# Moving one general path to the front of a branch in a mixture-of-experts kernel

## The chip, the cores and the metric

The kernel runs on one core of a Trainium2 chip. The core has a matrix engine (TensorE, PE in the rows), a vector engine (VectorE, DVE), a scalar engine (ScalarE, ACT), a general engine (GpSimd, POOL) and a sync engine (SyncE, SP) that issues most transfers. Each engine has an instruction queue of its own and runs through it in order; engines wait for one another by semaphores. The metric is the device time of one execution in microseconds (us), as the median of several.

## The reference

Two model blocks run one after the other on 256 tokens of width 1024. The first has a pooling and attention mixer and a gated feed-forward layer, the second a state-space and mLSTM mixer and then a hierarchical mixture of experts with 32 experts, of which each token takes two. The change concerns the experts:

```python
pg, g_sel = lax.top_k(p_group, 1)
e_in = jnp.take_along_axis(e_logits, g_sel[:, :, None], axis=1)[:, 0]
top_v, top_i = lax.top_k(e_in, TOP_K)
gates = jax.nn.softmax(top_v, axis=-1) * pg
ids = (g_sel * EXPERTS_PER_GROUP + top_i).reshape(-1).astype(jnp.int32)
order = jnp.argsort(ids)
tok = order // TOP_K
xs = xf[tok]
sizes = jnp.bincount(ids, length=N_EXPERTS).astype(jnp.int32)
hg = lax.ragged_dot(xs, w_gate.astype(xs.dtype), sizes)
hu = lax.ragged_dot(xs, w_up.astype(xs.dtype), sizes)
ys = lax.ragged_dot(jax.nn.silu(hg) * hu, w_down.astype(xs.dtype), sizes)
ys = ys * gates.reshape(-1)[order][:, None].astype(ys.dtype)
y = jax.ops.segment_sum(ys, tok, num_segments=t)
```

So for each expert the tokens that chose it are gathered, multiplied by its gate and up weights (1024 x 512 each) and its down weights (512 x 1024), scaled, and added back into the tokens' rows. How many tokens an expert gets is known only at run time. With these inputs 26 of the 32 experts get any; six of them get over 32 tokens (107, 85, 50, 50, 46 and 33), none over 256.

## The kernel before

Until about 555 us the dense parts run, as straight code. The expert stage that follows is in `experts`. The experts are put in an order at run time (`compact`): first those fixed at the front, whose weights are loaded early, then the rest, and the places are chosen so that a heavy expert stands second in a pair. The program runs over the pairs; `nest` stops it after the last expert that has tokens.

A **round** (`enter`) works on up to 32 tokens (CAP) of one expert: 16 products of the gathered tokens with the four gate and up weight tiles (L1851, into the PSUM tile gu or, for a further round, gx), with the turn (L1885, a transposition) and the down products (L1896) of the round before it woven in between; then ScalarE and VectorE form silu(gate) x up (L1867 to L1874), and TensorE adds the earlier round's result into the output sums (`flush`, L1799). Every four experts one `gather` (L1743, L1765, L1772) collects the tokens of their first 32 places. So the last half of a round is done within the next round.

A **pair** runs the first round of its experts a and b. Then `key[p]`, read from a tile by all engines, decides. If it is at most 32 (CAP), control goes to the Else of L2038, where SyncE issues the next weight loads. If it is over 32 (an *over pair*: here pairs 4 to 9) and at most 256 (T), the second expert's further rounds run (`rounds`, one after the other, each behind a test at L1960 whether there are more tokens, up to round RI = 4, and from there a general loop). If it is over 256, which the keys bring about only where the pair's *first* expert has over 32 tokens, the Else of L2039 runs the general path, `rest`: a loop with a run-time count, for a and for b. Here it never runs, but its code stands between the rounds and the join, and the rounds end with a jump over it. The tests of L2038 and L1960 have a branch hint, issued by `enter` early in the round (L1822); the test of L2039 has none.

The engines meet each of these tests separately, in their own queues. At a join every engine has to have its semaphore counts the same whichever way was taken; the way that leaves a block out sets marks for it.

`order` (L1690 to L1698) makes the keys: two very small products that carry the counts into the chosen order, and four VectorE instructions that write the tiles ce (counts) and ekey (keys). It runs in the first gather, ahead of its last part.

Of the kernel before, what the change touches and what calls it, by code (L numbers as in the profile page):

```python
# [16 lines left out]
ALU = mybir.AluOpType  # L17
# [8 lines left out]
T = 256  # L26
# [9 lines left out]
CAP = 32  # L36
# [62 lines left out]
class Kern:  # L99
# [1526 lines left out]
    def compact(self):  # L1626
# [13 lines left out]
        kt = self.ep.tile([1, NE // 2], F32, name="ekt", bufs=1)  # L1640
# [5 lines left out]
        V = nc.vector  # L1646
# [43 lines left out]
        def order():  # L1690
            for j, src in enumerate((cc, ec[:, 0:1])):
                nc.tensor.matmul(pp[0:1, 64 + 32 * j : 96 + 32 * j], src, P, start=False, stop=True, skip_group_check=True)
            V.tensor_copy(self.ce, pp[0:1, 64:128].rearrange("p (b e) -> p b e", b=2))

            first, second = (pp[0:1, 64:96].rearrange("p (q k) -> p k q", k=2)[:, j, :] for j in range(2))
            V.tensor_scalar(kt, first, float(CAP), 2.0 * T, op0=ALU.is_gt, op1=ALU.mult)
            V.tensor_tensor(kt, kt, first, ALU.max)
            V.tensor_tensor(self.key, kt, second, ALU.max)  # L1698

# [12 lines left out]
        def gates():  # L1712
            pg = self.pmi.tile([128, 512], F32, tag="mi", name="cmpg")
            nc.tensor.matmul(pg[0:NE, 0:T], P2, gT[0 : 64 + NE, :], start=True, stop=True, skip_group_check=True)
            self.split_gates(NE, pg)

        return sizes, places, order, moved, gates

    def gtile(self, name, shape, dt):
# [185 lines left out]
    def experts(self, st):  # L1905
        nc, tc = self.nc, self.tc
# [24 lines left out]
        sizes, places, order, moved, gates = self.compact()  # L1931
        parts = groups[0]
        chosen = parts[0]()
# [2 lines left out]
        self.counts()  # L1936
        places()
        parts[2]()
        order()
        parts[3]()  # L1940

        routing = {
            0: self.ranks, 1: lambda: self.gates(chosen),
        }

        def count(src, after=()):

            loads, vals = nc.values_load_multi_w_load_instructions(src, engines=[PE_, ACT_, DVE_, SP, POOL_])
            for ld in loads:
                for a in after:  # L1950
                    self.behind(ld, a)
            return vals[0], loads

        def loads(i, first, n):
            for q in range(6 * i + first, 6 * i + first + n):
                self.eload(NSLOT + q)

        def rounds(i, r, val, tag, prev, before=()):

            with tc.If(val > CAP * r, label=f"{tag}_{r}") if r > 1 else contextlib.nullcontext():  # L1960
                if r == RI:
                    end(i)
                    rest(i, r, val)
                    clear()
                    return
                n = CAP * (r + 1)

                odd = r % 2 == (0 if i < GR else 1)

                s0 = GR * CAP if i < GR else 2 * CAP * (i % GR)  # L1970
                xh = self.xs[:, :, s0 : s0 + 2 * CAP]
                if not odd:
                    for f in self.gather(i, 1, r, 2 * CAP, xh, selh):
                        f()
                xs = xh[:, :, CAP:] if odd else xh[:, :, 0:CAP]
                marks = self.enter(i, r, xs, {}, (f"{tag}_{r + 1}", val > n) if n < T else None, prev)
                for m in marks:
                    for b in before:
                        self.behind(m, b)
                rounds(i, r + 1, val, tag, i)  # L1980

        def end(i):

            self.turn()
            m = self.down(i)
            self.flush()
            return m

        def rest(i, r, val):

            ro = self.roff
            nc.vector.tensor_copy(ro[:, 0:1], self.iotap[:, r : r + 1])
            nc.vector.tensor_scalar(ro[:, 1:2], self.iotap[:, 0:1], 0.0, float(CAP * r), op0=ALU.mult, op1=ALU.add)
            s0 = GR * CAP if i < GR else 2 * CAP * (i % GR)
            xh = self.xs[:, :, s0 : s0 + CAP]
            with tc.For_i(CAP * r, val, CAP):
                for f in self.gather(i, 1, None, CAP, xh, selh[:, :, :, 0:CAP]):
                    f()
                self.enter(i, None, xh)
                end(i)  # L2000
                nc.vector.tensor_scalar(ro, ro, float(CAP), None, op0=ALU.add)

        def clear():

            for h in range(2):
                nc.vector.tensor_scalar(self.st[:, 128 * h : 128 * h + 128], self.ones, 0.0, None, op0=ALU.mult)

        key = {}
        self.ereg = None

        def pair(p):

            a, b = 2 * p, 2 * p + 1
            if a in groups and a:

                for f in groups[a][1:]:
                    f()
            for i in (a, b):
                s0 = CAP * i if i < GR else 2 * CAP * (i % GR)
                marks = self.enter(  # L2020
                    i, 0, self.xs[:, :, s0 : s0 + CAP], {} if i else routing,
                    (f"over{p}", key[p] > CAP if p else "LikelyTaken") if i == a else None, i - 1 if i else None,
                )
                if i == 0:
                    moved()
                    gates()
                    self.rank = self.rank2
                    key[0], _ = count(self.key[0:1, 0:1])
                if i == a and i:
                    loads(i - 1, 4, 2)  # L2030
            if b + 1 in groups:
                groups[b + 1][0]()
            before = ()
            if b + 1 < NE:
                key[p + 1], before = count(self.key[0:1, p + 1 : p + 2], marks)
            ereg = self.ereg

            with tc.If(key[p] > CAP, label=f"over{p}") as c:  # L2038
                with tc.If(key[p] <= T) as c2:  # L2039

                    loads(a, 0, 6)
                    rounds(b, 1, key[p], f"over{p}", b, before)
                    loads(b, 0, 4)
                with c2.Else():
                    self.ereg = ereg
                    ca, cb = (count(self.ce[0:1, 0, i : i + 1])[0] for i in (a, b))
                    end(b)
                    rest(a, 1, ca)
                    loads(a, 0, 6)
                    rest(b, 1, cb)  # L2050
                    clear()
                    loads(b, 0, 4)
            with c.Else():
                self.ereg = ereg
                loads(a, 0, 6)
                loads(b, 0, 4)
            self.ereg = None
# [11 lines left out]
        def nest(p):  # L2069

            if p == NE // 2:
                last(NE - 1)
                return
            with tc.If(key[p] > 0) as c:  # L2074
                pair(p)
                nest(p + 1)
            with c.Else():
                last(2 * p - 1)


        for p in range(GR // 2):
            pair(p)
# [247 lines left out]
```

## Time and profile before

| | |
|---|---|
| median of 3 runs | 1009.46 us (1008.82 to 1010.08) |
| the profiled execution | 1012.31 us |
| its span, first to last instruction | 1010.3 us |
| mean granted TensorE clock | 0.929 of full speed |
| TensorE busy | 889.5 us, 88% |
| VectorE busy | 581.9 us, 58% |
| ScalarE busy | 428.5 us, 42% |
| moved by DMA | 252.19 MB, 250 GB/s |

Busy time is the time in which an engine has an instruction in work; branches, semaphore instructions and register work don't count. A wait is the idle time ahead of an instruction, put down to what released it. "PEq", "DVEq" and "ACTq" are the instruction queues (sequencers) of the engines, whose branch instructions have rows of their own. A branch on PE that takes long shows in its duration; on ScalarE and VectorE the time shows between the compare and the next instruction of the queue.

### The profile page before, as it was taken

How to read it: one execution, taken by the hardware profiler on the slowest of the kernel's cores; microseconds unless marked ns; L12 is line 12 of the kernel's file. 1: busy time of each engine (PE TensorE's matmuls, PEld its weight loads, DVE VectorE, ACT ScalarE, POOL GpSimd, SP SyncE). 2: the span in 40 equal slices, each digit the busy share in tenths (PEclk: the TensorE clock that was granted, in tenths of full speed). 3: DMA queues.
4: the chain of work that ended last, by engine and by line, in shares of the span. 5: the costliest groups of instructions: out<-in, count | busy, mean ns of one | idle time of the engine just before them, and what ended most of it. 6: DMA issues, size and time to landing. Idle time of an engine off the chain costs nothing. (4 is left out here: it accounts for less than half of the span.)

```text
span 1010.3 us, 17831 instructions
## 1 busy us (share of the span) xinstructions
PE 889.5 (88%) x6738; PEld 655.6 (65%) x6738; DVE 581.9 (58%) x1203; ACT 428.5 (42%) x788; POOL 135.4 (13%) x160
## 2 busy tenths in 40 slices
PE   7989999999999899999999888788687977797973
PEld 7969899999998799889998323244234323224332
DVE  6777888777776999988974432332232322323322
ACT  5445566655573656765545221211221321322313
POOL 3440331111115400161230000000000000000000
PEclk9999999999998999999999898887797987987987
DMA  8533445555564345435777599999484798997951
GB/s 341 204 119 126 167 159 189 208 198 202 179 235 177 126 151 191 160 116 199 291 291 264 199 407 418 423 417 415 179 334 169 316 363 330 374 378 296 390 239 48
DMA packets 36323, 252.19 MB, mean 250 GB/s; under 512 B 4144, under 2 KB 4272, under 8 KB 6320
## 3 DMA queue, kind: packets, MB, share of 16 engines
q1 hardware_dynamic: 35712, 249.51, 63.9%
q8 instruction: 83, 1.36, 0.5%
q14 instruction: 96, 0.79, 0.2%
q10 hardware_dynamic: 432, 0.53, 0.1%
HBM read 269.95 MB, written 1.05 MB: 268 GB/s over the span
## 5 line engine op out<-in xcount | busy, mean ns | idle before, releaser
L136 DVE TENSOR_TENSOR wlo<-ring,whi 128x1024 fp32r<-128x1024 f32 (+1 forms) x157 | 197.6, 1260 | 43.3 <-ACT whi L134 41.5
L134 ACT ACTIVATE whi<-ring 128x1024 fp32r<-128x1024 f32 (+1 forms) x160 | 167.7, 1052 | 123.1 <-PE up L153 19.1
L1902 DVE TENSOR_TENSOR y<-py,y 128x512 fp32r<-128x512 f32 x35 | 24.2, 692 | 192.4 <-ACT y L1901 184.5
L1851 PE MATMUL gu<-early,xs 128*32 128x512 f32 x472 | 81.0, 649 | 3.3 <-DVE ez L1868 3.3
L1765 PE MATMUL xsp<-sel,H 128*128 128x256 f32 (+1 forms) x224 | 41.3, 359 | 40.1 <-issue 20.9
L1886 ACT ACTIVATE hT<-py 128x128 f32<-128x128 f32 x35 | 9.7, 278 | 155.7 <-PE py L1885 155.7
L1851 PE MATMUL gu<-ring,xs 128*32 128x512 f32 x336 | 62.1, 638 | 10.3 <-issue 7.5
L1765 PEld LDWEIGHTS xsp<-sel,H 128*128 128x128 f32 x224 | 39.2, 268 | 43.2 <-issue 22.1
L1901 ACT ACTIVATE y<-py 128x512 fp32r<-128x512 f32 x35 | 20.9, 598 | 93.9 <-PE py L1896 93.9
L1772 DVE TENSOR_TENSOR xs<-xsp,gn 128x512 f32<-128x512 f32 (+1 forms) x30 | 19.1, 637 | 65.0 <-PE xsp L1765 48.2
L1851 PE MATMUL gu<-ringc,xs 128*32 128x512 f32 x160 | 34.5, 709 | 16.3 <-DMA ring<-in_we_dram 14.8
L152 PE MATMUL dn<-ah,whi 128*128 128x256 f32 x176 | 48.6, 276 | 0.0
L153 PE MATMUL dn<-al,whi 128*128 128x256 f32 x176 | 48.6, 276 | 0.0
L154 PE MATMUL dn<-ah,wlo 128*128 128x256 f32 x176 | 48.6, 276 | 0.0
L739 POOL TENSOR_TENSOR av<-sg,cc 128x256 f32<-128x256 f32 x22 | 30.5, 1387 | 126.7 <-ACT sg L737 126.2
L1799 PEld LDWEIGHTS eacc<-y,oneh 64*128 64x128 f32 x280 | 23.9, 188 | 34.9 <-ACT ez L1838 26.8
L1799 PE MATMUL eacc<-y,oneh 64*128 64x512 f32 x280 | 43.2, 426 | 1.3 <-ACT y L1901 1.2
L1868 DVE TENSOR_TENSOR ez<-gu,ez 64x512 f32<-64x512 f32 x35 | 23.9, 683 | 25.7 <-ACT ez L1867 25.5
L1885 PEld LDWEIGHTS py<-idr,ez 32*128 32x128 f32 x140 | 12.0, 145 | 40.4 <-issue 28.7
L732 DVE SCALAR_TENSOR_TENSOR cc<-u,cpack,cc 128x255 f32<-128x255 f32 (+1 forms) x88 | 37.4, 485 | 0.2
L1869 ACT ACTIVATE esz<-ez,col 32x512 f32<-32x512 f32 x35 | 25.2, 721 | 25.5 <-DVE ez L1868 25.5
L1874 DVE SCALAR_TENSOR_TENSOR ez<-ez,col,esz 32x512 f32<-32x512 f32 x35 | 25.9, 741 | 13.2 <-ACT esz L1869 10.7
(1220 smaller groups left out, 2693.8 us busy)
## 6 DMA issues: line engine op xcount, KB each, us to landing
ring<-in_wd_dram SPq DMA_DIRECT2D x77, 1024.0 KB
early<-in_we_dram SPq DMA_DIRECT2D x72, 1024.0 KB
ring<-in_we_dram SPq DMA_DIRECT2D x48, 1024.0 KB
ringc<-in_we_dram SPq DMA_DIRECT2D x32, 1024.0 KB
ringb<-in_we_dram SPq DMA_DIRECT2D x16, 1024.0 KB
xbuf<-in_we_dram SPq DMA_DIRECT2D x8, 1024.0 KB
ring<-in_wd_dram SPq DMA_DIRECT2D x4, 512.0 KB
xbuf<-in_xT_dram SPq DMA_DIRECT2D x4, 256.0 KB
```

Of the source, the lines that this page charges most:

```text
L134: nc.scalar.activation(hf[:, c], src[:, c], AF.Copy)
L136: eng.tensor_tensor(lf[:, c], src[:, c], hf[:, c].bitcast(F32), ALU.subtract)
L152: nc.tensor.matmul(ps, hi[:, j, :], xh, start=start, stop=False, skip_group_check=True)
L153: nc.tensor.matmul(ps, hi[:, j, :], xl, start=False, stop=False, skip_group_check=True)
L154: nc.tensor.matmul(ps, lo[:, j, :], xh, start=False, stop=stop, skip_group_check=True)
L732: nc.vector.scalar_tensor_tensor(cc[:, s, sh:T], in0=u[:, s, 0 : T - sh], scalar=self.c("cw", tap * 44 + m), in1=cc[:, s, sh:T], op0=ALU.m ...
L739: nc.gpsimd.tensor_tensor(a, sg, cc[:, 1, :], ALU.mult)
L1765: m = nc.tensor.matmul(ps[:, c * n * S : (c + 1) * n * S], self.H[j][:, b, ch], sel[:, b].rearrange("p k s -> p (k s)"), start=(b == 0 and ...
L1799: self.nc.tensor.matmul(self.sums[b][h], self.st[rows, b * 128 : b * 128 + 128], y[rows, :], start=False, stop=False, skip_group_check=True,)
L1851: m1 = nc.tensor.matmul(gu[32 * t : 32 * t + 32, :], xs[:, 4 * (t // 2) + kc, :], w[t][:, 512 * kc : 512 * kc + 512], start=(kc == 0), sto ...
L1869: nc.scalar.activation(self.sz[32:64, :], z[0:32, :], AF.Silu, scale=col[0:32, :])
L1874: m2 = nc.vector.scalar_tensor_tensor(z[32:64, :], in0=z[32:64, :], scalar=col[32:64, :], in1=self.sz[32:64, :], op0=ALU.mult, op1=ALU.mult)
```

## The change

Three edits in `experts` and `compact`:

- The general path for a full first expert moves from the Else behind the second expert's rounds to an If of its own in front of them. It now holds only the part for a: the end of b's first round, the loop over a's tokens, and a clearing of a tile. The rounds of b follow in either case; where b has over 128 tokens, the general loop in `rounds` takes it, as before.
- The key of a pair whose first expert has over 32 tokens is 257 (T + 1) instead of 512 (2 T).
- `order()` is called in the first expert's first round, behind its first four products and behind `ranks`, instead of ahead of the last part of the first gather.

```diff
-            V.tensor_scalar(kt, first, float(CAP), 2.0 * T, op0=ALU.is_gt, op1=ALU.mult)
+            V.tensor_scalar(kt, first, float(CAP), T + 1.0, op0=ALU.is_gt, op1=ALU.mult)
...
         parts[2]()
-        order()
         parts[3]()
...
-            0: self.ranks, 1: lambda: self.gates(chosen),
+            0: lambda: (self.ranks(), order()), 1: lambda: self.gates(chosen),
...
             with tc.If(key[p] > CAP, label=f"over{p}") as c:
-                with tc.If(key[p] <= T) as c2:
-
-                    loads(a, 0, 6)
-                    rounds(b, 1, key[p], f"over{p}", b, before)
-                    loads(b, 0, 4)
-                with c2.Else():
-                    self.ereg = ereg
-                    ca, cb = (count(self.ce[0:1, 0, i : i + 1])[0] for i in (a, b))
+
+                with tc.If(key[p] > T):
+                    ca, _ = count(self.ce[0:1, 0, a : a + 1])
                     end(b)
                     rest(a, 1, ca)
-                    loads(a, 0, 6)
-                    rest(b, 1, cb)
                     clear()
-                    loads(b, 0, 4)
+                loads(a, 0, 6)
+                rounds(b, 1, key[p], f"over{p}", b, before)
+                loads(b, 0, 4)
```

The lines of the kernel after are up to six less than these (L2038 is L2037, L1960 is L1959, L1996 is L1995); the inner If is L2039 in both. The whole program gets shorter: TensorE's order falls from 12328 rows to 11114, VectorE's from 2588 to 2270, ScalarE's from 2030 to 1808.

TensorE's order at the end of the first gather before (xsp is the gather's result, rankp the tile of the keys, gu the first expert's first product):

```order
L1765 MATMUL xsp_4_7002<-sel,H_6522 128x128
L1692 MATMUL rankp<-eperm,ccol 1x32
L1692 MATMUL rankp<-eperm,ecol 1x32
L1765 MATMUL xsp_4_7002<-sel,H_6523 128x128
...
L1851 MATMUL gu_7023<-early_3697,xs 32x512
L1851 MATMUL gu_7023<-early_3693,xs 32x512
L1851 MATMUL gu_7023<-early_3694,xs 32x512
L1851 MATMUL gu_7023<-early_3698,xs 32x512
L2325 BRANCH_PREFETCH_HINT
```

The same place after:

```order
L1765 MATMUL xsp_4_6996<-sel,H_6523 128x128
L1851 MATMUL gu_7017<-early_3697,xs 32x512
L1851 MATMUL gu_7017<-early_3693,xs 32x512
L1851 MATMUL gu_7017<-early_3694,xs 32x512
L1851 MATMUL gu_7017<-early_3698,xs 32x512
L2319 BRANCH_PREFETCH_HINT
L1692 MATMUL rankp<-eperm,ccol 1x32
L1692 MATMUL rankp<-eperm,ecol 1x32
```

The two key products moved behind five gather products and four expert products.

TensorE's order at the start of an over pair's rounds before, here pair 5, with the semaphores that a row waits for (gu_11420 is the first extra round's product; DVE_49 and Activation_49 are set by VectorE and ScalarE):

```order
L1799 MATMUL eacc_6043<-y_6936,oneh 128x512
L1948 TENSOR_LOAD ekey
L2038 COMPARE_AND_BRANCH
L2039 COMPARE_AND_BRANCH
L1851 MATMUL gu_11420<-early_3697,xs 32x512
L1851 MATMUL gu_11420<-early_3693,xs 32x512
```

After, with the block of the general path, whose first row stands behind the compare and which 93 rows later ends ahead of the products:

```order
L1947 TENSOR_LOAD ekey
L2037 COMPARE_AND_BRANCH
L2039 COMPARE_AND_BRANCH
L1885 MATMUL py_10732<-idr,ez 128x32 [waits DVE_49,PE_49]
...
L2039 UNCONDITIONAL_BRANCH
L2039 UNCONDITIONAL_BRANCH [waits PE_49,PE_sequencer_49]
L1851 MATMUL gu_10877<-early_3697,xs 32x512 [waits DVE_49,PE_49,Activation_49]
L1851 MATMUL gu_10877<-early_3693,xs 32x512
```

The general block moved from behind the rounds to ahead of them, and the round's first product has waits for three semaphores that it did not have.

At the end of the same pair's rounds, TensorE before: the way with rounds jumps from the first L2039 row over the Else of 168 rows:

```order
L1960 UNCONDITIONAL_BRANCH
L1960 UNCONDITIONAL_BRANCH [waits PE_49] x3
L2039 UNCONDITIONAL_BRANCH [waits PE_sequencer_49]
L1885 MATMUL py_11805<-idr,ez 128x32 [waits DVE_49,PE_49]
...
L2039 UNCONDITIONAL_BRANCH
L2038 UNCONDITIONAL_BRANCH [waits PE_49,PE_sequencer_49]
L2074 COMPARE_AND_BRANCH
```

After, the Else is gone and the rounds end at the join:

```order
L1959 UNCONDITIONAL_BRANCH
L1959 UNCONDITIONAL_BRANCH [waits PE_49] x3
L2037 UNCONDITIONAL_BRANCH
L2037 UNCONDITIONAL_BRANCH [waits PE_49,PE_sequencer_49]
L2068 COMPARE_AND_BRANCH
```

What stood between the rounds and the join is one general body less in each pair, and none of it is behind the rounds now. Counted in rows from the compare of L2038 to the end of its block, ScalarE's order of an over pair falls from 74 to 60 and VectorE's from 97 to 77; the general block itself is 16 rows on ScalarE and 22 on VectorE.

## Rows read from the trace of the kernel before

**Rows 1.** Stretches without TensorE work after the over pairs: us, busy time by engine, PEclk, DMA.

```profile
...
807.01:814.22 7.21, 0.00 (x0) 0.00 (x1) 2.33 (x5) 1.12 (x3) 0.00 (x0) 0.83 1.01 403
...
sum 43.04, PE 0.01 PEld 0.01 DVE 11.72 ACT 6.75 POOL 0.00; mean PE 0.00 PEld 0.00 DVE 1.95 ACT 1.12 POOL 0.00
```

**Rows 2.** Instructions of L2039, pair 6: duration ns min/median/max, first and last start.

```profile
L2039 PEldq COMPARE_BRANCH  x2: 67/3110/6153, 798.2 to 807.7; - x2
```

**Rows 3.** Waits of PE, 595 to 990 us: total us, times, longest us.

```profile
PE xsp L1765 <- DVEq L2038: 16.7, 3, 5.6
```

**Rows 4.** Instructions of L2038 at the end of pair 1.

```profile
L2038 ACTq EVENT_SEMAPHORE  x2: 17/17/17, 608.9 to 609.0; - x2
L2038 ACTq COMPARE_BRANCH  x1: 49/49/49, 603.5 to 603.5; - x1
```

**Rows 5.** Timeline, TensorE: start, us, what, [idle before <-releaser].

```profile
561.86 0.21 PE L1692 MATMUL rankp<-eperm,ccol 32*1 32x32 f32 x2 [2.36 <-DVE eperm L1686]
562.06 0.84 PE L1765 MATMUL xsp<-sel,H 128*128 128x128 f32 x5
...
594.82 1.92 PE L1851 MATMUL gu<-ringc,xs 128*32 128x512 f32 x16 [1.05 <-issue]
...
603.28 1.17 PE L1765 MATMUL xsp<-sel,H 128*128 128x256 f32 x8 [0.65 <-DVE ez L1868]
...
691.83 1.43 PE L1765 MATMUL xsp<-selh,H 128*128 128x64 f32 x8 [2.58 <-DVE selh L1743]
```

**Rows 6.** Timeline, the extra round of pair 6.

```profile
798.88 1.92 PE L1851 MATMUL gu<-ring,xs 128*32 128x512 f32 x16
...
800.20 0.74 DVE L1874 SCALAR_TENSOR_TENSOR ez<-ez,col,esz 32x512 f32<-32x512 f32 x1 [0.40 <-ACT esz L1869]
...
801.09 0.40 PE L1885 MATMUL py<-idr,ez 32*128 32x32 f32 x4 [0.29 <-DVE ez L1874]
```

**Rows 7.** Granted clock after three gaps of TensorE.

```profile
692.30:702.60 10.30, 10.30 (x48) 7.20 (x47) 0.85 (x2) 0.00 (x0) 0.00 (x0) 0.50 1.02 430
562.60:566.00 3.40, 3.40 (x19) 1.23 (x17) 0.35 (x3) 1.14 (x4) 0.00 (x0) 0.50 0.02 5
593.80:600.50 6.70, 5.68 (x51) 1.89 (x55) 1.82 (x3) 1.73 (x4) 0.00 (x0) 1.00 1.02 423
```

**Rows 8.** Instructions of L1960 on PE, pairs 4 and 6 to 9.

```profile
L1960 PEldq COMPARE_BRANCH  x1: 346/346/346, 715.5 to 715.5; - x1
...
L1960 PEldq COMPARE_BRANCH  x1: 1617/1617/1617, 805.7 to 805.7; - x1
...
L1960 PEldq COMPARE_BRANCH  x1: 2467/2467/2467, 839.1 to 839.1; - x1
...
L1960 PEldq COMPARE_BRANCH  x1: 3019/3019/3019, 876.5 to 876.5; - x1
...
L1960 PEldq COMPARE_BRANCH  x1: 1663/1663/1663, 910.5 to 910.5; - x1
```

**Rows 9.** Stretches of single rounds (first four) and gathers (last two).

```profile
698.30:707.30 9.00, 9.00 (x58) 2.69 (x57) 1.33 (x3) 1.25 (x3) 0.00 (x0) 0.76 0.92 390
724.30:733.60 9.30, 9.30 (x57) 2.50 (x57) 0.96 (x2) 1.25 (x3) 0.00 (x0) 0.70 0.57 213
814.20:822.90 8.70, 8.65 (x57) 2.40 (x57) 0.91 (x2) 1.25 (x3) 0.00 (x0) 0.75 0.77 288
853.70:860.40 6.70, 6.70 (x58) 2.00 (x57) 1.67 (x3) 1.25 (x3) 0.00 (x0) 1.00 0.19 57
918.88:925.30 6.42, 6.39 (x32) 6.30 (x32) 2.07 (x3) 0.00 (x0) 0.00 (x0) 0.57 0.93 385
610.00:614.70 4.70, 4.67 (x24) 4.60 (x24) 2.08 (x3) 0.00 (x0) 0.00 (x0) 0.59 1.02 420
```

**Rows 10.** The page, part 3.

```profile
q8 instruction: 83, 1.36, 0.5%
```

**Rows 11.** Busy time and DMA share, 750 to 800 us.

```profile
750.00:800.00 50.00, 40.05 (x273) 21.79 (x277) 14.02 (x31) 9.44 (x20) 0.00 (x0) 0.83 0.51 205
```

## The prediction

> **What bounds the kernel now.** The page's busy shares come first, in the table above: TensorE works for 88% of the span, so what counts is when it does nothing and when it runs at the lower clock. The change acts in the expert stage (555 to 990 us), so I read TensorE's gaps there, then the branch instructions of the lines that the diff moves, then the timeline around them.
>
> With these inputs no expert has more than 256 tokens and no first expert of a pair more than 32, so the general path never runs, before or after. What the change can alter is only which code is jumped over, where, and who waits where the two ways meet. Pairs 4 to 9 take the way with extra rounds ("over pairs": three rounds, two, and four times one); pairs 0 to 3 and 10 to 12 do not. Three kinds of stall stand out.
>
> First, the end of each over pair: TensorE does nothing for 43.0 us in six gaps of about 7 us [rows 1]. In each its sequencer is inside the branch of L2039, the jump from the end of the rounds over the Else with the two general bodies. In pair 6 that branch took 6.15 us; falling through at the start of the rounds it took 0.067 us [rows 2]. (The profile puts this gap on a weight transfer. The branch begun at 807.7 us is in flight until 813.9, so I put it on the branch.)
>
> Second, after pairs 1, 3 and 11 TensorE waits 16.7 us for VectorE, which is held behind L2038 [rows 3]. These pairs jump over the whole extra-round block: in pair 1 ScalarE starts its compare at 603.5 us and reaches the next instruction at 608.9 us [rows 4].
>
> Third, 2.36 us before order()'s two small products, which wait for the permutation made by VectorE [rows 5].
>
> **The change part by part.**
>
> *order() moved.* Before, its products stand ahead of the last five gather products, so these (0.84 us) and all first expert products wait with them [rows 5]. After, VectorE's chain ends no earlier, but the five and four of the first products are done inside the wait. Eight such products take 1.92 us [rows 6], four about 0.96: -1.8 us. Bounds: 0 (they wait for ScalarE's copies instead) and -4.1, the whole wait and the 1.7 us that the lower clock behind it costs (3.4 us at 0.50 [rows 7]). The keys are written about as late as before; the first compare that needs them, pair 0's, comes some 20 us later and hides that.
>
> *End jump of the over pairs.* The Else is gone; the rounds end at the join. What remains is the hinted jump out of the rounds (L1960). It ends 0.3, 1.2, 1.7 and 0.3 us after the last flush in pairs 6 to 9 (start plus duration in [rows 8], less the gap's start: 807.01 in [rows 1], and 840.40, 877.85 and 911.83 us for those not printed), and before the flush in pairs 4 and 5: 3.5 us. For the compares and semaphores of each join I add 0.6 us, an estimate from the 0.65 us ahead of the gather at 603.28 us [rows 5]. 43.0 - 3.5 - 3.6 = 35.9: -35.9 us.
>
> *New start jump.* A jump over one general body now stands ahead of the first extra round, on every engine. For TensorE the nearest row is the jump of pair 4 at 715.5 us, which also passes one general body: 0.346 us [rows 8]. The other end is the old end jump over two bodies, 6.15 us. The passed block is 93 rows of TensorE's order instead of 168, so I take the short one, but an even chance of a miss in two of the six pairs, since hinted jumps out of the rounds, longer ones, took 1.6 to 3.0 us [rows 8]. A miss costs 6.15 less the 2.3 us that the next wait hides, 3.8: +3.8.
>
> *New wait.* Before, pair 6's extra round started at 798.88 us, with nothing to wait for, and its products ran beside VectorE's L1874 (until 800.20 + 0.74 = 800.94 us), so the turn at 801.09 us was hardly late [rows 6]. After, the first product writes a buffer that the skipped body also uses. It waits for the marks that VectorE and ScalarE set for that body, and these come behind L1874 in their queues. It starts at about 801.2 us, 2.3 us late, of which 0.3 us come back at the turn: +2.0 per over pair. On TensorE the whole round is queued behind it. The lower end is 0, if the marks were there already, the upper 7.6 (rival D).
>
> *The clock.* A gap of 2.3 us has a second price. [...] Together 4.3 x 6 = +25.8 us.
>
> The same term pays back where a gap of 7 us becomes one of about 1 us. The products after pairs 4 and 6 took 9.3 and 8.7 us against 6.7: -4.6. The gather after pair 9 took 6.42 us at 0.57, at full clock about 3.7: -2.7 [rows 9]; pair 5's in the same way -2.0; pair 7 keeps the longer gap of 1.8 us, so half, -1.3; pair 8, with 2.3 us, nothing. Sum -10.6.
>
> *Stalls of pairs 1, 3 and 11.* The block to be jumped over loses a general body: on ScalarE it falls from 74 rows to 60, on VectorE from 97 to 77. Pairs 0, 2, 10 and 12 pass the same jump without a stall, so its length must be near a limit set by where the code lies. I take it that all three go, down to the 0.65 us of [rows 5]: -16.7 + 1.9 = -14.8. The gather behind pair 1 took 4.70 us at 0.59 [rows 9], at full clock 2.8; of these 1.9 us each I count two thirds: -4.0. Ends: 0 and -20.5.
>
> [...]
>
> *The rest.* The key's new constant costs the same instruction. SyncE passes one more jump ahead of the weight loads; the transfers run far ahead (the DMA engines stand at 0.51 of their time from 750 to 800 us [rows 11], for want of free buffers). Without that cover each us of SyncE's delay would count.
>
> Sum: -1.8 - 35.9 + 3.8 + 25.8 - 10.6 - 14.8 - 4.0 = -37.5 us. The profiled execution took 1012.3 us, 2.8 above the median of 1009.5: 974.8 for a profiled run, **972.0 us** for the median.
>
> **The rivals.**
>
> A. *The clock holds in the extra rounds.* The 1.05-us gap without a drop speaks for it, those of 2.36 and 2.58 us against. 6 x 2.3 = 13.8 us less: 958.2 us.
>
> B. *The stalls after pairs 1, 3 and 11 stay*, there or at other pairs. For: they strike by position. Against: the block shrinks by a fifth. +18.8: 990.8 us.
>
> C. *TensorE's new start jump misses in all six pairs.* For: it has no hint, and the old one without a hint missed each time. Against: about half the length, and 0.346 us for the like jump. One miss is in the sum; five more at 3.8 us: 991.0 us. With B: 1009.8 us, no change.
>
> [...]
>
> D. *Slower: ScalarE and VectorE miss at the new jump as at L2038.* They take it right after L1874, and TensorE's round waits for their marks. At 5.4 us (608.9 - 603.5) the round starts at 806.5 instead of 801.2 us: 5.3 x 6 = 31.8 us; TensorE's own miss is hidden then (-3.8); and if such jumps still miss, B holds too (+18.8). 972.0 + 46.8 = 1018.8 us. It decides from 37.5 / 6 = 6.2 us per over pair, with B from 3.1 us. For: no hint there either. Against: a body is 16 rows on ScalarE and 22 on VectorE, under a third of what is passed at L2038.
>
> E. *The weights become the bound.* Against: [rows 11]. Were half the gain lost so, 991 us.
>
> **How the numbers follow.** Forecast 0.45, A 0.15, B 0.14, C 0.12, B with C 0.04, D 0.08, E 0.02. Faster by over 0.2% (about what a measurement of this kernel can tell): forecast, A, B, C and E, 0.88; within 0.2%: B with C, 0.04; slower: D, 0.08. The range of 8 in 10 reaches from below A, by the 2.3 us that order() and some 8 us that start jump and gathers may still give (948), to above B and C by some us (998). The forecast's own range is 960 to 984.
>
> **What would show it.** Right: no branch over 4 us at the end of the over pairs, and gaps of 1 to 2 us there; ahead of each first extra round a gap of 2.2 to 2.4 us, ended by VectorE or ScalarE, with a granted clock of 0.50 behind it; no gap over 5 us after pairs 1, 3 and 11. Wrong: branches of 6 us at the inner If on TensorE (C), extra rounds 7 us late with ScalarE and VectorE held at that branch (D), gaps of 5.5 us at other pairs (B), first products that wait for transfers (E).

## The result

The kernel after took 973.02 us (median of 4 runs, 970.86 to 974.64), the kernel before 1009.77 us in the same session (1008.82 to 1010.71): a ratio of 0.9635, 95% interval 0.9614 to 0.9656, or -36.8 us. The forecast was 972.0 us, with a range of 948 to 998. The profiled run took 973.01 us with a span of 971.1 us, 39.2 us shorter than before (the profiled run before took 1012.31 us and lies 2.5 us above its median, so the spans differ by more than the medians); TensorE's mean granted clock rose from 0.929 to 0.958.

The ends of the over pairs, which stood in [rows 1], answer with these stretches without TensorE work (the columns are the same: length, busy time by engine, PEclk, DMA share, GB/s):

```profile
708.75:709.74 0.99, 0.00 (x0) 0.00 (x0) 0.83 (x2) 0.52 (x1) 0.00 (x0) 1.00 0.08 33
...
816.32:817.75 1.43, 0.00 (x1) 0.01 (x1) 1.03 (x3) 0.72 (x1) 0.00 (x0) 1.00 1.02 424
...
sum 6.09, PE 0.01 PEld 0.01 DVE 5.10 ACT 3.03 POOL 0.00; mean PE 0.00 PEld 0.00 DVE 0.85 ACT 0.50 POOL 0.00
```

43.0 us in six gaps have become 6.1. Ahead of the extra rounds there are six new ones, in the same view:

```profile
672.56:674.96 2.40, 0.00 (x0) 0.00 (x0) 1.60 (x3) 0.92 (x2) 0.00 (x0) 1.00 1.01 416
...
776.13:778.30 2.17, 0.00 (x1) 0.00 (x0) 1.60 (x3) 0.92 (x2) 0.00 (x0) 1.00 0.53 98
...
839.03:842.46 3.43, 0.00 (x1) 0.00 (x1) 1.60 (x3) 0.93 (x2) 0.00 (x0) 0.82 0.13 48
...
sum 14.73, PE 0.01 PEld 0.01 DVE 9.58 ACT 5.54 POOL 0.00; mean PE 0.00 PEld 0.00 DVE 1.60 ACT 0.92 POOL 0.00
```

In all six VectorE is busy for 1.6 us: it finishes the last round, L1874 included, before its mark releases TensorE. The waits of the expert stage name it, and show what became of [rows 3] (16.7 us):

```profile
PE gu L1851 <- DVEq L2039: 11.5, 5, 2.4
...
PE xsp L1765 <- DVEq L2037: 1.7, 3, 0.6
```

The waits are five; the gap left over, in pair 8, ends with TensorE's own start jump. Of TensorE's six branches at the inner If four took 0.33 to 0.43 us, pair 9's 2.03 us (hidden in the wait) and pair 8's 3.72 us. Pair 6's and pair 8's:

```profile
L2039 PEldq COMPARE_BRANCH  x1: 331/331/331, 775.4 to 775.4; - x1
...
L2039 PEldq COMPARE_BRANCH  x1: 3722/3722/3722, 838.3 to 838.3; - x1
```

So far as forecast. The timeline of the tenth expert's round (a row with DMA in its brackets waited for a weight transfer) shows what was not:

```profile
659.76 1.10 PE L1851 MATMUL gu<-ringb,xs 128*32 128x512 f32 x4 [0.46 <-DVE ez L1868]
662.29 1.05 PE L1851 MATMUL gu<-ring,xs 128*32 128x512 f32 x2 [1.43 <-DMA ring<-in_we_dram]
664.78 0.62 PE L1851 MATMUL gu<-ring,xs 128*32 128x512 f32 x1 [1.44 <-DMA ring<-in_we_dram]
```

The round waits for its third and its fourth weight tile, 2.5 us apart, and the last expert with tokens does the same at 935.7 and 938.2 us. The two rounds take 11.6 and 11.7 us instead of 6.7. The DMA engines were full up to both: their share is 1.01 from 600 to 670 us and from 900 to 935 us.

```profile
600.00:670.00 70.00, 62.65 (x484) 25.07 (x476) 23.74 (x47) 16.92 (x38) 0.00 (x0) 0.98 1.01 421
```

### The profile page after: what moved, and what is told of

It is laid out like the page before. It is cut to its first block, busy times and chain, and to the rows that moved or that the text cites. A ratio compares the mean times of both kernels' runs of the same rounds, so it can differ in the third digit from the quotient of the medians.

```text
span 971.1 us, 17861 instructions
## 1 busy us (share of the span) xinstructions
PE 882.4 (91%) x6738; PEld 642.6 (66%) x6738; DVE 582.7 (60%) x1203; ACT 428.7 (44%) x788; POOL 134.2 (14%) x160
## 5 line engine op out<-in xcount | busy, mean ns | idle before, releaser
L1851 PE MATMUL gu<-ring,xs 128*32 128x512 f32 x336 | 64.1, 647 | 15.5 <-PEq L2039 3.5
L1799 PEld LDWEIGHTS eacc<-y,oneh 64*128 64x128 f32 x280 | 23.4, 184 | 34.8 <-ACT ez L1838 27.7
L1799 PE MATMUL eacc<-y,oneh 64*128 64x512 f32 x280 | 42.4, 419 | 1.3 <-ACT y L1901 1.3
L1851 PE MATMUL gu<-ringc,xs 128*32 128x512 f32 x160 | 32.1, 642 | 6.7 <-DMA ringc<-in_we_dram 2.8
L1851 PEld LDWEIGHTS gu<-early,xs 128*32 128x32 f32 x472 | 14.6, 114 | 31.9 <-issue 15.1
L1765 PE MATMUL xsp<-sel,H 128*128 128x256 f32 (+1 forms) x224 | 28.7, 281 | 7.5 <-DVE oneh L1873 1.9
L1874 DVE SCALAR_TENSOR_TENSOR ez<-ez,col,esz 32x512 f32<-32x512 f32 x35 | 25.9, 741 | 13.5 <-ACT esz L1869 9.5
L1765 PEld LDWEIGHTS xsp<-sel,H 128*128 128x128 f32 x224 | 26.6, 188 | 10.9 <-ACT ez L1867 3.1
```

Of the source, the lines that this page charges most:

```text
L1765: m = nc.tensor.matmul(ps[:, c * n * S : (c + 1) * n * S], self.H[j][:, b, ch], sel[:, b].rearrange("p k s -> p (k s)"), start=(b == 0 and ...
L1799: self.nc.tensor.matmul(self.sums[b][h], self.st[rows, b * 128 : b * 128 + 128], y[rows, :], start=False, stop=False, skip_group_check=True,)
L1851: m1 = nc.tensor.matmul(gu[32 * t : 32 * t + 32, :], xs[:, 4 * (t // 2) + kc, :], w[t][:, 512 * kc : 512 * kc + 512], start=(kc == 0), sto ...
L1874: m2 = nc.vector.scalar_tensor_tensor(z[32:64, :], in0=z[32:64, :], scalar=col[32:64, :], in1=self.sz[32:64, :], op0=ALU.mult, op1=ALU.mult)
```

## The experiments

**The new wait.** In this kernel, called own_psum, the general path's round writes the PSUM tile that a pair's first rounds use:

```diff
-        gu = self.pgu.tile([128, 512], F32, tag="gu" if r == 0 else "gx", name=f"gu{u}")
+        gu = self.pgu.tile([128, 512], F32, tag="gx" if r else "gu", name=f"gu{u}")
```

> The kernel after, but a round of the general loop writes its first product into the PSUM tile gu instead of gx, so that the skipped block no longer touches the tile of the extra rounds. Theory (the new wait is for the marks of that block): the gaps of 2.2 to 2.4 us ahead of the six extra rounds go, about 2.0 us each, so at first sight 12 us; but the weights already hold the 10th and the 26th expert back by about 5 us each, and part of what is gained between these two is lost at the second: 960 to 966 us. Rival 1 (the wait comes with the join itself, whatever tile): no change, 973 us. Rival 2 (the wait moves to the next pair's first product, which writes gu): no change in sum, gaps of about 2 us at the ends of the over pairs instead.

987.55 us, ratio to before 0.976 (0.9707 to 0.9814): slower than the kernel after. The waits ahead of the extra rounds went, and the wait for the marks turned up ahead of the next pair's first product or gather, also behind pairs without extra rounds. Seven of these gaps, those up to the third over pair:

```profile
578.59:581.94 3.35, 0.00 (x1) 0.00 (x0) 1.54 (x3) 1.12 (x3) 0.00 (x0) 0.97 1.02 426
599.61:601.96 2.35, 0.00 (x1) 0.00 (x0) 1.60 (x3) 1.13 (x3) 0.00 (x0) 1.00 1.02 429
...
sum 17.43, PE 0.01 PEld 0.01 DVE 11.28 ACT 7.88 POOL 0.00; mean PE 0.00 PEld 0.00 DVE 1.61 ACT 1.12 POOL 0.00
```

That is rival 2, and more of it than expected. It shows what the wait is in these kernels: the first instruction to touch a tile that a skipped block would have written waits for that block's marks, with 1.6 us of VectorE's work in it on average, as in the kernel after. Not all of the 987.55 us is this wait: TensorE's jumps were slower too (pair 9's start jump took 3.5 us for 2.0 in the kernel after, the one out of pair 7's rounds 6.2 for 2.1).

So the next kernel, py_psum, gives that round the tile that every round touches only in its turn:

```diff
+        pool, tag = (self.ppy, "py") if r is None else (self.pgu, "gx" if r else "gu")
-        gu = self.pgu.tile([128, 512], F32, tag="gu" if r == 0 else "gx", name=f"gu{u}")
+        gu = pool.tile([128, 512], F32, tag=tag, name=f"gu{u}")
```

> The kernel after, but a round of the general loop writes its first product into the PSUM tile py, which every round touches only in its turn, after VectorE's L1874 anyway. Theory (the wait moved in the run with gu because gu is the first thing that the next pair's round writes; py is not): no wait of 2 us ahead of the extra rounds and none in its place at the ends of the pairs: 958 to 966 us, near the kernel without the front block. Rival (any tile that the skipped block writes makes some engine wait for its marks, now in the gathers): 970 to 985 us.

980.48 us, ratio 0.9706 (0.9674 to 0.9737). The wait is gone from the starts and has not moved, as the theory says, and still the kernel is slower than the one after; the time is in the rival's range, but not by its mechanism. What was gained came back in and behind the rounds, most of it at the jumps out of them. Pairs 6 and 7 of this kernel:

```profile
L1960 PEldq COMPARE_BRANCH  x1: 6052/6052/6052, 776.9 to 776.9; - x1
...
L1960 PEldq COMPARE_BRANCH  x1: 5830/5830/5830, 809.0 to 809.0; - x1
```

In the kernel after they took 1.62 and 2.07 us. The start jumps of pairs 8 and 9 (3.71 and 3.75 us) have no wait to hide them either, and behind these pairs TensorE stood still for 3.5 us twice more. The hint of pair 6 was given at 769.9 us, during a transfer of instructions (769.71 to 771.02 us), and from then until the jump itself at 776.9 us no further packet of instructions came. So the hint may have been lost in that transfer. Giving the hint later tests that:

```diff
-            if kc == 0:
+            if kc == (2 if r == 1 else 0):
                 ahead(m1, PE_)
```

> The run with the PSUM tile py, with TensorE's branch hint in a first extra round given behind its third group of products instead of its first. In the run with py the hint of pair 6 came at 769.87 us, within the code fetch of the start jump (769.71 to 771.02 us), no second fetch followed, and the jump out of the rounds took 6.1 us; in the kernel after the wait for the marks put the hint at 778.45 us, behind that fetch, and the jump took 1.6 us. Theory (a hint given during a fetch is lost): the jumps out of the rounds in pairs 6 and 7 fall from 5.8 to 6.1 us to 1 to 3.5 us, the gaps behind them from 5.2 and 5.6 us to under 3 us: 968 to 975 us. Rival (the jump is slow because the round is 2 us shorter behind the start jump, wherever the hint is): no change, about 980 us.

981.48 us, ratio 0.9734 (0.9712 to 0.9756). Pair 6's jump fell to 2.7 us as the theory asked, pair 7's stayed at 6.2:

```profile
L1960 PEldq COMPARE_BRANCH  x1: 2668/2668/2668, 776.7 to 776.7; - x1
...
L1960 PEldq COMPARE_BRANCH  x1: 6216/6216/6216, 807.3 to 807.3; - x1
```

So a hint lost in a transfer explains at most one of the two jumps, and the time did not fall. Two more kernels went on from there, both with the later hint. One adds a label and a hint for the start jump (`tc.If(key[p] > T, label=f"full{p}")`), the other, for the stall of 2.7 us ahead of the gather after pair 11 in py_psum, moves the hint for L2038 to the pair's second expert (`if i == b`).

> As the run before this one, with a hint for the start jump too, given in the first round of the pair's second expert. Theory: the start jumps of pairs 8 and 9 fall from 3.7 us to about 0.4 us: 6 to 7 us less than with the late hint alone, 962 to 968 us. [...]

> As the run with py and the late hint, with the hint for the test of L2038 given in the second expert's first round instead of the first's, about 8 us nearer to the test, on all engines. [...]

980.16 us (ratio 0.9735, 0.9679 to 0.9791) and 981.9 us (0.9724, 0.97 to 0.9748): neither gains. With the extra hint the start jumps of pairs 8 and 9 still took 3.4 us each; with the hint of L2038 moved the stall ahead of the gather after pair 11 was still there (two gaps, 1.7 and 1.3 us). And py_hint_b speaks against the lost hint in pair 6 as well: its hint there came at 780.1 us, 1.6 us behind the transfer (777.43 to 778.54 us), and the jump was slow again:

```profile
L1960 PEldq COMPARE_BRANCH  x1: 6327/6327/6327, 784.3 to 784.3; - x1
```

In the kernel after, too, no packet of instructions followed pair 6's hint (778.5 us) until 783.9 us, and its jump took 1.62 us. What makes these jumps slow or quick stays open.

**What the front block costs in sum.** The kernel after without the block:

```diff
-                with tc.If(key[p] > T):
-                    ca, _ = count(self.ce[0:1, 0, a : a + 1])
-                    end(b)
-                    rest(a, 1, ca)
-                    clear()
```

> The kernel after without the general path for a full first expert (left out; with these inputs it never runs). Neither a jump nor a join ahead of the extra rounds. Theory: all that the front block costs goes, that is the wait (2.0 us in six pairs), the two slow start jumps (1.4 us beyond the wait in pair 8) and the lower clock behind them in pairs 5, 8 and 9 (1.6, 2.6 and 1.5 us), 19 us in sum, of which the wait for weights at the 26th expert takes some back: 955 to 962 us. Rival (the front block costs only the jump): 970 us.

962.16 us, ratio 0.9509 (0.9478 to 0.9541), against 0.9635 for the kernel after: without the block the time is lower by 1.3% of 1009.8 us, about 13 us; 19 were summed up for it. That sum was right at its own place: from the TensorE products that add up the earlier round (L1799) to the next such products, the six first extra rounds with their gaps took 48.4 us in this trace and 68.4 us in that of the kernel after, 20.0 us less. But there are new stalls of 4.3, 5.6 and 4.4 us behind pairs 2, 3 and 11, and they cost more than the end of the waits for weights gave back. So the 13 us are a balance and not the price of the block alone. The jumps out of the rounds were at most 1.9 us there:

```profile
L1959 PEldq COMPARE_BRANCH  x11: 67/361/1857, 680.8 to 860.3; - x11
```

**Length or place.** One body behind the rounds in the kernel before, and two ahead of them in the kernel after:

```diff
 (before)
                     rest(a, 1, ca)
                     loads(a, 0, 6)
-                    rest(b, 1, cb)
                     clear()
 (after)
                     rest(a, 1, ca)
+                    rest(a, 1, ca)
                     clear()
```

> The kernel before, with one general body instead of two in the Else behind the rounds (the second expert's general loop is left out there; it never runs). The end jump is as long as the new start jump of the kernel after (one body), the block of L2038 is as short, but nothing stands ahead of the extra rounds. Theory by length (a jump is slow when it leaves the code that is held): end branches of 0.3 to 2 us, no stall after pairs 1, 3 and 11, no wait ahead of the extra rounds: 953 to 965 us, faster than the kernel after. Rival by place (a jump without hint at the end of the rounds always misses): end branches of 5 to 6 us stay, only the stalls of pairs 1, 3 and 11 go: about 995 us.

> The kernel after with the general loop of the first expert written twice in the front block (it never runs), so that the start jump passes two bodies and the block of L2037 is as long as before. Theory by length: TensorE's start branch takes about 6 us in all six pairs (3.7 us more than the wait it hides in pairs 4 to 7, 2.4 and 4 in 8 and 9), the clock falls behind it, and the stalls of about 5.5 us after pairs 1, 3 and 11 are back, while the waits for weights at the 10th expert go: 1000 to 1015 us. Rival by place (a start jump is short wherever it stands, and the odd pairs' stalls came from the Else): 973 to 980 us.

992.4 us, ratio 0.9805 (0.9754 to 0.9855), and 990.3 us, 0.9799 (0.9734 to 0.9863): each between what its two theories gave. TensorE's branches at the inner If, short_else (six short ones at the start, six end jumps) and two_in_front (six start jumps):

```profile
L2039 PEldq COMPARE_BRANCH  x12: 67/976/4344, 674.0 to 899.0; - x12
```

```profile
L2039 PEldq COMPARE_BRANCH  x6: 3568/3721/5957, 670.6 to 885.7; - x6
```

Both theories hold half. With length, at one place: two bodies instead of one raise the start jump from mostly 0.33 to 0.43 us to 3.6 us or more, and one instead of two lowers the end jump from 5.1 to 6.4 us to 1.9 to 4.3. With place, at one length: one body costs 0.33 to 0.43 us ahead of the rounds in four pairs of six and at least 1.9 us behind them, where it follows another jump directly. The change gained by both. In two_in_front the stalls came back after pairs 1 and 11, not after pair 3:

```profile
PE xsp L1765 <- DVEq L2037: 6.3, 2, 5.7
...
PE xsp L1765 <- ACTq L2037: 4.4, 1, 4.4
```

**The three stalls.** In no_front_block, where the block of L2037 is shortest, two of these stalls are there too, after pairs 3 and 11 (5.6 and 4.4 us). In short_else, whose block is as short as in the kernel after, there is none after pair 1, but 2.5 and 2.1 us stand after pairs 3 and 11. So length alone does not rule them. The last kernel shifts the code of VectorE and ScalarE, by 60 instructions in pair 0's front block, which is never run; behind pair 0 all lengths stay as they are:

```diff
+                    for _ in range(60 if p == 0 else 0):
+                        nc.vector.tensor_copy(self.roff[:, 0:1], self.iotap[:, 1:2])
+                        nc.scalar.activation(self.warm[:, 0:1], self.warm[:, 1:2], AF.Copy)
                     ca, _ = count(self.ce[0:1, 0, a : a + 1])
```

> [...] Theory of the prediction (the block of L2037 is now short enough): no stall of ScalarE or VectorE after pairs 1, 3 and 11, at most one after pair 0, 970 to 979 us. Rival (whether a jump stalls hangs on where the code lies; the kernel after has a lucky position): stalls of 4 to 6 us after one or more of pairs 1, 2, 3, 10, 11 and 12, 978 to 990 us.

969.88 us, ratio 0.9623 (0.9594 to 0.9651). A stall after pair 1 is back, 5.6 us, on VectorE:

```profile
L2037 DVEq EVENT_SEMAPHORE  x2: 21/21/21, 613.1 to 613.2; - x2
...
L2037 DVEq COMPARE_BRANCH  x1: 72/72/72, 607.4 to 607.4; - x1
```

So the stall goes with the place of the code, as far as one trace shows it, and the kernel after has a good one. TensorE's code was not moved in this run, and yet its jump out of pair 9's rounds took 6.1 us for 1.6 in the kernel after, so place does not explain every jump:

```profile
L1959 PEldq COMPARE_BRANCH  x1: 6122/6122/6122, 877.7 to 877.7; - x1
```

The time did not rise all the same. The tenth expert's round, begun 4.7 us later than in the kernel after, found its weights there and ended at 671.1 us, for 671.4 there:

```profile
664.47 0.62 PE L1851 MATMUL gu<-ringb,xs 128*32 128x512 f32 x2 [0.46 <-DVE ez L1868]
664.49 0.62 PE L1851 MATMUL gu<-ring,xs 128*32 128x512 f32 x2
```

**The weights.** The kernel after, loading only half of some weight tiles; it leaves out the other half and so measures time alone:

```diff
+            if i in (4, 5, 6, 7, 8, 20, 21, 22, 23, 24):
+                slot, src = slot[:, 0:1024], src[:, 0:1024]
             nc.sync.dma_start(slot, src, cond=cnt > 0, cond_hint=True)
```

> The kernel after, loading only half of each weight tile of the experts in places 4 to 8 and 20 to 24 (the other half is left out), so that the weights of the 10th and 26th expert are there early; computation and order are unchanged. Theory (these two wait for their weights): the gaps of 1.3 to 1.4 us in their first products go and both rounds fall from 11.6 to about 6.7 us: 963 us. If the DMA engines also hold up the fetch of instructions, the code stalls in the lightened stretches get shorter as well (the 3.0 us after 586 us, the 3.4 us at 839 us is outside): 958 to 961 us. Rival (these gaps are code being fetched): no change, 973 us.

956.77 us, ratio 0.9489 (0.9461 to 0.9517). Both rounds fell to 6.7 us:

```profile
649.50:656.20 6.70, 6.70 (x57) 1.99 (x59) 2.00 (x4) 1.90 (x4) 0.00 (x0) 1.00 1.01 423
918.50:925.20 6.70, 6.67 (x57) 1.98 (x57) 1.99 (x4) 1.94 (x4) 0.00 (x0) 1.00 0.00 0
```

The weights hold the kernel after back at these two places. The two rounds account for 9.9 of the 14.7 us (0.0146 of 1009.8). Most of the rest is the clock: from 580 to 600 us it was 1.00 here and 0.80 in the kernel after, and the third and fourth experts' rounds took 4.7 us less. The stall behind 580 us itself stayed (2.8 us for 3.0) with the DMA share there down from 0.91 to 0.73. Pair 8's of 3.4 us stayed too; it lies where few transfers ran in the kernel after already (share 0.13 in the gap).

**The two edits apart.** One kernel has only order() moved, one only the If (the diff's second and third part, and its first and last).

> The kernel before with only order() moved. Theory: the five gather products and the first four expert products go into the wait for the permutation: 1.8 us less at 560 us, unless the positions of the code change other stalls, which they should not, since the program has the same length and order elsewhere: ratio 0.998, the gap of 2.36 us shorter by about 1.4 us. Rival (the products now wait for ScalarE's copies): 1.000.

> The kernel after with order() back at its old place, so only the If is moved. Theory: the If carries all but some 2 us: 1.8 us above the kernel after, ratio to before about 0.966. Gaps of 2.2 to 2.4 us ahead of the extra rounds as there. Rival (the earlier start of the first expert is what the rest hangs on): over 0.975.

1002.58 us, ratio 0.9928 (0.9907 to 0.9948), and 977.68 us, 0.9671 (0.9641 to 0.9701). Alone, order() brought 7 us instead of 1.8, in two places. At its own it brought 3.3 us, counted from the first gather's start: the 2.36 us of [rows 5] became 0.37, and the clock behind them was 1.00 where [rows 7] had 0.50:

```profile
562.60:566.00 3.40, 3.40 (x24) 0.75 (x20) 0.42 (x1) 0.75 (x2) 0.00 (x0) 1.00 0.01 5
630.00:643.00 13.00, 11.27 (x93) 3.54 (x92) 3.42 (x8) 3.01 (x7) 0.00 (x0) 1.00 1.01 422
```

The second row covers pair 3, where the kernel before had a gap of 2.00 us that no wait explains and 6.8 us at a clock of 0.50 from 637.7 us. Here the gap is 1.27 us and the clock 1.00, another 3.3 us:

```profile
632.49 1.93 PE L1896 MATMUL py<-ring,hT 128*32 128x512 f32 x16 [1.27 <-issue]
```

That the order of 560 us shortens a gap at 632 us was seen, not explained. The If alone carries most of the change; between if_alone and the kernel after the intervals overlap.

These two kernels also tell how far one trace per kernel goes. Ahead of the expert stage, where no edit reaches, the traces differ: the first gather begins at 557.3 us in the kernel after and at 562.4 us in if_alone. Behind it the stalls repeat: apart from the gap ahead of order()'s products, every TensorE gap of over 2 us in one of these two traces is in the other as well, within 0.3 us.

## Why the prediction was right

It named 972.0 us and the time was 973.0. The runs bear out the mechanism of the large terms at the over pairs. That the sum came within 1 us is luck: the clock in the extra rounds was counted 8 us too dear, the weights were put at nothing and cost 9.9 us, and these errors cancel.

*The end jumps* (-35.9): 43.0 to 6.1 us, -36.9. The residue of about 1 us per pair was right.

*Start jump and wait* (six gaps of 2.3 us and 3.8 us for misses, 17.6): 14.7. The misses came in pairs 8 and 9, but pair 9's was hidden by the wait, and that the wait is for marks of the skipped block was shown by moving it.

*The clock in the extra rounds* (+13.8) was, of the terms counted, the one furthest off. No run shows the 2.3 us that the sum takes for each of the six rounds; the trace of the kernel after shows 1.6, 2.6 and 1.5 us in pairs 5, 8 and 9. The clock fell in pairs 5 and 9 (0.79 and 0.81 over the round), behind gaps of 2.17 and 2.40 us, and in pair 8 (0.70), behind 3.43 us; in pairs 4, 6 and 7 it was 1.00 behind gaps of 2.16 to 2.40 us:

```profile
675.00:681.70 6.70, 6.70 (x57) 2.05 (x57) 0.96 (x2) 1.26 (x3) 0.00 (x0) 1.00 1.02 418
728.00:736.30 8.30, 8.26 (x57) 2.38 (x57) 0.94 (x2) 1.25 (x3) 0.00 (x0) 0.79 0.98 389
...
sum 46.80, PE 46.01 PEld 13.34 DVE 5.64 ACT 7.52 POOL 0.00; mean PE 7.67 PEld 2.22 DVE 0.94 ACT 1.25 POOL 0.00
```

46.8 us less six times 6.7 are 6.6 us. Of these 0.9 are not the clock: pair 7's round took 7.6 us at a clock of 1.00, with a stall of 0.7 us in it. So the clock cost 5.7 us instead of 13.8: more than half of rival A came true. The give-back behind the over pairs (-10.6) was -11.2, but not piece by piece: 27.0 to 22.1 us in the three rounds after pairs 4, 6 and 8, 18.5 to 12.2 in the three gathers (the clock in the six was 0.57 to 0.75 before and 1.00 after). The round after pair 6 took 8.8 us (8.7 before), now at a clock of 1.00 for 0.75, with a stall of 1.1 us in it; the one after pair 8, counted with nothing, gave 2.3.

*The stalls of pairs 1, 3 and 11* (-14.8 and -4.0) went, 16.7 to 1.7 us, and the gathers behind them fell from 14.6 to 8.7 us. The size was right and the reason was not: a block short enough fell with the runs no_front_block and short_else, and shifted points to the place of the code. What the shorter block adds to that is open.

*The weights.* This step failed: "the transfers run far ahead", read from a share of 0.51 between 750 and 800 us [rows 11]. It was the wrong stretch. The stalls that were to go lay at 605 and 655 us, ahead of a stretch where the DMA engines were full in the kernel before as well:

```profile
600.00:650.00 50.00, 40.58 (x287) 16.86 (x286) 15.31 (x30) 11.32 (x25) 0.00 (x0) 0.86 1.01 419
650.00:700.00 50.00, 40.42 (x279) 21.97 (x281) 15.74 (x33) 10.47 (x23) 0.00 (x0) 0.85 1.01 422
```

With them gone, the tenth expert began 13.6 us earlier, while its weight loads were issued 1.3 us earlier (636.9 for 638.2 us). Rival E, which had a chance of 0.02, came true for 9.9 us.

*order()* (-1.8): the first expert begins 1.5 us earlier and the second 2.0, although the first gather began 1.4 us later in this trace (557.26 for 555.89 us). So the edit brought 3.4 us here, 2.0 of the gap and the rest of the clock of 0.50 behind it, as the bound of -4.1 allowed. Alone it is worth 7.

The terms measured, with the two rounds above, are -2.0 - 36.9 + 14.7 - 1.8 (the turn) + 6.6 - 11.2 - 15.0 - 5.9 + 9.9 = -41.6 us; the span fell by 39.2. Three stretches stand in no term of the prediction. In pair 1 a stall of 3.0 us that no wait explains (585.86 to 588.88 us) and the clock behind it (0.50 from there to 595.5 us) cost 7.4 us. In pair 3 the gap of 2.0 us and the clock of 0.50 behind it went, -4.7. The gathers in the second extra rounds of pairs 4 and 5 fell from 6.6 and 6.9 to 5.0 us each, at a clock of 0.72 for 0.54 and 0.51, -3.3. That makes -42.2; the 3 us that are left were not assigned.

## What to carry over

A branch that is never taken is not free: it costs where its code lies in the way (here 5.1 to 6.4 us with two bodies behind the rounds, 1.9 to 4.3 with one there, mostly 0.33 to 0.43 with one ahead of them), and at the join the first instruction that touches what the skipped block would have written waits for the slowest engine's mark (here 2.2 to 2.4 us in five over pairs, VectorE's work of 1.6 us in it). When a stall is taken out, look at the transfers in the stretch right behind it, not at the average of a later one. And a gain at one stall can return at the next jump, as in py_psum: the wait of 2.2 us looked like pure loss, and without it the time rose (980.48 us for 973.02). That the wait had covered the fetching of code was not shown.

No version tried that keeps the general path is clearly faster than the kernel after (shifted lies within its interval); without the front block some 13 us more went.

## What the runs showed that was not expected

The same gap can keep or drop the clock: after 2.40 us ahead of pair 4's extra round it was 1.00, after 2.17 us ahead of pair 5's it was 0.79 over the round. What decides that, no run shows. And two stalls of 5.6 and 5.5 us (the second at a jump of 6.1 us out of pair 9's rounds) in the run shifted left its time within the interval of the kernel after, since both lay ahead of a round that had waited for weights.
